# One hybrid decoder step on one core: the last layer's down projection with 512 weight columns moving past stationary activations

## The chip, the core and the metric

The kernel runs on one NeuronCore of a Trainium2 chip. TensorE (PE in the rows, with its weight loads as PEld) multiplies, VectorE (DVE), ScalarE (ACT) and GpSimd (POOL) work on vectors, SyncE (SP) issues most transfers. The metric is the device time of one execution in microseconds. The kernel before takes 2923.28 us, the median of three runs (2923.02 to 2924.85).

## What is computed

The reference is one step of a two-layer decoder on 320 tokens: 256 of a prompt and 64 of eight samples. Each layer has a mixer and a feed-forward part. The part that matters here is the feed-forward of the second (last) layer, whose result is the output:

```python
def _ffn(h, w1, w2):
    a = jax.nn.relu(jnp.einsum('btd,df->btf', h, w1))
    return jnp.einsum('btf,fd->btd', a * a, w2)

y_p = y_p + _ffn(_rmsnorm(y_p, norm_ffn[li]), w_ff1[li], w_ff2[li])
y_s = y_s + _ffn(_rmsnorm(y_s, norm_ffn[li]), w_ff1[li], w_ff2[li])
```

D_MODEL is 2048 and the hidden size 8192, so w1 is 2048 x 8192 and w2 8192 x 2048, both in f32.

## The kernel before

Activations lie transposed: 128 channels on the partitions, 16 chunks of channels, and the 320 tokens (N) in the free dimension. Every f32 product is made of three products of float32r numbers (fp32r in the rows): each operand is split into a high part h and a remainder l, and l·h + h·l + h·h is summed in PSUM. xh, xl hold the hidden activations of a quarter, yh, yl the normed input of a layer, y the residual.

Weights come in units of 2 x 128 rows by 512 columns (w_dma, SP, tile wraw, four buffers). w_conv makes of each half unit (128 rows x 512 columns) whi on ACT (line 145) and wlo on DVE (line 146), six buffers each; w_fill keeps six halves converted or in use and is called once for every two halves, before their matmuls.

gemm is the loop of every large product. A group is 512 output columns in four PSUM banks of six (m = 0 to 3); for every pair of k chunks (a step of two halves) and each m it issues, per chunk, three matmuls: 128 weight columns are stationary, the 320 tokens move (lines 204 to 206). So one chunk and one group are 12 matmuls of 320 moving columns. After the last chunk of a bank comes evac. Work around it is hung on two counters: after(k, f) runs f k calls of step() later (a step() after each m), at(n, f) at slot n (side() counts one slot per pair of halves).

ffn(l, ...) goes through the hidden dimension in four quarters: up (w1, reads yh and yl, evac writes xh and xl), then down (w2, reads xh and xl). In each down, residual multiplies the bank by r1 (line 1455, DVE; r1 is the squared norm's reciprocal per token, the same on all partitions) and adds it to y (POOL at line 1459, one step later, or DVE at 1457 in the last quarter of the last layer). In that last quarter store turns each finished chunk of y: three transposes on TensorE into a bank (line 1634), a copy of the prompt's part by ACT (1635) and of the samples' by DVE (1636), and for every second chunk two transfers out (1640, 1641).

The order of every engine's instructions is the order in which the program issues them; nothing reorders them later.

Of the kernel before, what the change touches and what calls it, by code (L numbers as in the profile page):

```python
# [11 lines left out]
F32 = mybir.dt.float32  # L12
F32R = mybir.dt.float32r
I32 = mybir.dt.int32
AF = mybir.ActivationFunctionType
ALU = mybir.AluOpType
AX = mybir.AxisListType

D = 2048
NP_TOK = 256  # L20
NB = 8
NT = 8
N = NP_TOK + NB * NT
# [47 lines left out]
def tile_hybrid_step(ctx: ExitStack, tc: tile.TileContext, A, O, stop=None, dbg=None):  # L71
    nc = tc.nc
    ctx.enter_context(tc.manual_schedule())
    V, S, G, PE, SP = nc.vector, nc.scalar, nc.gpsimd, nc.tensor, nc.sync
# [8 lines left out]
    def pool(name, side="left"):  # L83
        return tc.tile_pool(name=name, bufs=1, side=side, reuse_waits="tile")

    def bank(tag):
        return psum.tile([128, 512], F32, name="ps_" + tag, tag=tag, bufs=nbank[tag])
# [39 lines left out]
    st = {"dma": 0, "conv": 0, "half": 0, "step": 0, "slot": 0, "ahead": 2}  # L127

    def w_dma():
        w, k, ku, c, width = units[st["dma"]]  # L130
        st["dma"] += 1
        r = wp.tile([128, UW], F32, name="wraw", bufs=NRAW)
        SP.dma_start(r[:, :ku * width].rearrange("p (k f) -> p k f", k=ku),
                     w[k * 128:(k + ku) * 128, c:c + width].rearrange("(k p) f -> p k f", p=128))
        raws.append(r)

    def w_conv():
        u, hf = divmod(st["conv"], 2)
        if st["dma"] == u:
            w_dma()  # L140
        st["conv"] += 1
        r = (raws.popleft() if hf else raws[0])[:, hf * HW:hf * HW + HW]
        h = wp.tile([128, HW], F32R, name="whi", bufs=NSP)
        l = wp.tile([128, HW], F32R, name="wlo", bufs=NSP)
        S.copy(h, r)  # L145
        (G if u < 4 and hf == 0 else V).tensor_tensor(l, r, h.bitcast(F32), ALU.subtract)  # L146
        convs.append((h, l))

    def w_fill():
        while st["conv"] < min(st["half"] + st["ahead"], 2 * len(units)):  # L150
            w_conv()
        while st["dma"] < min(st["conv"] // 2 + NRAW, len(units)):
            w_dma()

    def w_next():
        ku, width = units[st["half"] // 2][2::2]
        ku //= 2
        st["half"] += 1
        h, l = convs.popleft()
        return (h.rearrange("p (k f) -> p k f", k=ku), l.rearrange("p (k f) -> p k f", k=ku), ku)  # L160
# [4 lines left out]
    def at(n, f, *a):  # L165
        later.setdefault(n, deque()).append((f, a))

    def side(n=1):
        st["slot"] += n
        n = st["slot"]  # L170
        for m in sorted(k for k in later if k <= n):
            q = later.pop(m)
            while q:
                f, a = q.popleft()
                f(*a)
# [4 lines left out]
    def after(k, f):  # L180
        dq.setdefault(st["step"] + k, []).append(f)

    def step():
        st["step"] += 1
        for k in sorted(k for k in dq if k <= st["step"]):
            for f in dq.pop(k):
                f()

    def gemm(groups, nk, act, evac, width=512):

        nm = width // 128
        for g in range(groups):
            ps = [bank("g") for _ in range(nm)]
            k = 0
            while k < nk:
                for nh in (2,) if width == 512 else (1, 1):
                    w_fill()
                    ks = [(h, l, j) for h, l, n in [w_next() for _ in range(nh)] for j in range(n)]
                    ku = len(ks)
                    for m in range(nm):  # L200
                        for j, (h, l, jj) in enumerate(ks):
                            ah, al = act(k + j)
                            wh, wl = h[:, jj, m * 128:(m + 1) * 128], l[:, jj, m * 128:(m + 1) * 128]
                            PE.matmul(ps[m][:, :N], wh, al, start=k + j == 0, stop=False)  # L204
                            PE.matmul(ps[m][:, :N], wl, ah, start=False, stop=False)  # L205
                            PE.matmul(ps[m][:, :N], wh, ah, start=False, stop=k + j == nk - 1)  # L206
                        if k + ku == nk:
                            evac(g, m, ps[m])
                        step()
                    k += ku  # L210
                side()
                yield

    def run(gen):
        for _ in gen:
            pass

    def drain():
        while dq:
            step()  # L220
# [3 lines left out]
    ident = cm[:, C_ID:C_ID + 128]  # L224
# [45 lines left out]
    tn = [128, 128, 64]  # L270
# [150 lines left out]
    def norm_begin():  # L421
        nacc["t"] = misc.tile([128, N], F32, name="nacc", bufs=2)
        nacc["n"] = 0
# [518 lines left out]
    for bp in range(4):  # L942
        for i in range(2):
            n = CN + 8 * bp + 4 * i
# [16 lines left out]
    for b in "sw":  # L961
        n = E["k" + b]
# [4 lines left out]
    for g in range(4):  # L967
        n = E[f"q{g}"]
# [4 lines left out]
    n = CN + 34  # L973
# [384 lines left out]
    for pr in range(4):  # L1358
        n = C0 + 8 * pr
# [14 lines left out]
    for b in range(NB + 1):  # L1374
        n = P4 + 3 * b
# [21 lines left out]
    actp = ctx.enter_context(ExitStack())  # L1397
    act = actp.enter_context(pool("act"))

    xh = act.tile([128, 16, N], F32R, name="xh")  # L1400
    xl = act.tile([128, 16, N], F32R, name="xl")
    y = ctx.enter_context(pool("ypl")).tile([128, 16, N], F32, name="y")
    for c in range(4):
        SP.dma_start(y[:, 4 * c:4 * c + 4], xt_d[:, 4 * c:4 * c + 4])
# [3 lines left out]
    n = st["slot"]  # L1408
# [28 lines left out]
    misc = ctx.enter_context(pool("misc", "right"))  # L1437
    r1 = misc.tile([128, N], F32, name="r1")
# [10 lines left out]
    def residual(ps, c, nxt, scale=None, last=False):  # L1449

        if scale is None:
            V.tensor_tensor(y[:, c], ps[:, :N], y[:, c], ALU.add)
        else:
            t = misc.tile([128, N], F32, name="rs", bufs=3)
            V.tensor_tensor(t, ps[:, :N], scale, ALU.mult)  # L1455
            if last or nxt is not None:
                V.tensor_tensor(y[:, c], y[:, c], t, ALU.add)
            else:
                after(1, lambda: G.tensor_tensor(y[:, c], y[:, c], t, ALU.add))  # L1459
        if nxt is not None:  # L1460
            if c == 0:
                norm_begin()

            gn = par[:, nxt + c:nxt + c + 1]

            def lo():
                V.scalar_tensor_tensor(yl[:, c], y[:, c], gn, yh[:, c].bitcast(F32), op0=ALU.mult, op1=ALU.subtract)

            after(1, lambda: S.activation(yh[:, c], y[:, c], AF.Copy, scale=gn))
            after(2, lambda: norm_add(y[:, c]))  # L1470
            after(3, lo)

    def after_norm(dst, squared):
        n = st["slot"]
        at(n + 2, norm_end, dst, squared)
# [2 lines left out]
        drain()  # L1478
        run(gemm(4, 16 - k0, lambda k: xact(k0 + k), lambda g, m, ps: residual(ps, 4 * g + m, nxt)))

    def ffn(l, nxt, last=None):
        def up(g, m, ps):
            c = 4 * g + m
            t = misc.tile([128, N], F32, name="fr", tag="fr", bufs=5)
            S.activation(t, ps[:, :N], AF.Relu)  # L1485

            def lo():
                V.tensor_tensor(t, t, t, ALU.mult)  # L1488
                V.tensor_tensor(xl[:, c], t, xh[:, c].bitcast(F32), ALU.subtract)  # L1489

            after(1, lambda: S.activation(xh[:, c], t, AF.Square))  # L1491
            after(3, lo)

        for qt in range(4):
            if qt == 0:
                drain()
                after_norm(r1, True)
            run(gemm(4, 16, yact2, up))
            drain()
            end = qt == 3  # L1500

            def down(g, m, ps):
                done = end and last is not None
                residual(ps, 4 * g + m, nxt if end else None, r1, done)
                if done:
                    after(3, lambda: last(4 * g + m))

            run(gemm(4, 16, xact, down))
        drain()

    GFF, GMX = GF, GM
    for qt in range(4):
# [108 lines left out]
        return  # L1621


    outp = ctx.enter_context(pool("outp"))
    yt = {}

    def store(c):
        q = c // 4
        if c % 4 == 0:
            yt[q] = outp.tile([128, 3, 512], F32, name="yt", bufs=2)  # L1630
        t = yt[q]
        p = bank("a")
        for i in range(3):
            PE.transpose(p[:tn[i], 128 * i:128 * i + 128], y[:, c, 128 * i:128 * i + tn[i]], ident)
        S.copy(t[:, 0:2, 128 * (c % 4):128 * (c % 4) + 128], p[:, :256].rearrange("p (i d) -> p i d", i=2))
        V.tensor_copy(t[:64, 2, 128 * (c % 4):128 * (c % 4) + 128], p[:64, 256:384])
        if c % 2:
            f = slice(128 * (c % 4) - 128, 128 * (c % 4) + 128)
            d = slice(128 * c - 128, 128 * c + 128)
            SP.dma_start(O[0][0].rearrange("(i p) d -> p i d", p=128)[:, :, d], t[:, 0:2, f])  # L1640
            SP.dma_start(O[1].rearrange("b t d -> (b t) d")[:, d], t[:64, 2, f])

    ffn(1, None, store)


# [28 lines left out]
```

## Time and profile before

| | us |
|---|---|
| median of three runs | 2923.28 |
| the profiled execution, device time | 2929.41 |
| its span (first to last instruction) | 2927.6 |
| TensorE matmul busy | 2872.9 (98%) |
| TensorE weight load busy | 2802.8 (96%) |
| VectorE busy | 1583.7 (54%) |
| ScalarE busy | 1256.6 (43%) |
| GpSimd busy | 285.6 (10%) |

The last layer's feed-forward takes the end of the span, from about 2015 us on. In the timeline a row has the start, the time taken, the engine, the line, the operation and its tiles; for a matmul `128*128 128x320` is the stationary tile (partitions * columns) and the moving one. Matmuls are pipelined: one shown with 0.31 us overlaps the next, and what counts is the distance from one start to the next. A merged row (x8) runs from the first start to the last end.

### The profile page before, as it was taken

Reading aid. Unit: us, or ns where it says so; the run is one execution under the profiler, and the core shown is the slowest. Engines: PE = TensorE matmul, PEld = TensorE weight load, DVE = VectorE, ACT = ScalarE, POOL = GpSimd, SP = SyncE. Lnnn points to the kernel's source line nnn. Section 1 sums busy time; section 2 is a strip of 40 time slices with the busy share of each in tenths; the row PEclk is TensorE's granted clock in tenths of the full one; section 3 lists DMA queues with packets and bytes.
Section 4 is the critical chain, followed back from the end, with each engine's and each line's share of the span. In section 5 each row is a group of like instructions: output and inputs, shape, how many; then the busy total and the mean of one; then the engine's idle time right before and its main releaser. Section 6 shows DMA issues by size and latency. Waiting matters only on the chain.

```text
span 2927.6 us, 53019 instructions
## 1 busy us (share of the span) xinstructions
PE 2872.9 (98%) x20723; PEld 2802.8 (96%) x20723; DVE 1583.7 (54%) x2913; ACT 1256.6 (43%) x2370; POOL 285.6 (10%) x449
## 2 busy tenths in 40 slices
PE   9998998999999999999999999999999999999999
PEld 8887777899999999999999999999999999999999
DVE  6676676665545444444565555555444444544544
ACT  5665754444434434433444333344433433433433
POOL 1103321020010010010010111111011011001000
PEclk9999999999999999999999999999999999999999
DMA  8765247645455555545444444444545544444543
GB/s 242 213 202 149 73 142 227 218 139 149 161 166 165 159 163 161 166 159 165 149 147 153 151 148 149 151 148 148 153 149 148 150 150 153 149 149 150 149 157 120
DMA packets 284826, 463.94 MB, mean 158 GB/s; under 512 B 18666, under 2 KB 112598, under 8 KB 284047
## 3 DMA queue, kind: packets, MB, share of 16 engines
q1 hardware_dynamic: 281886, 453.68, 50.4%
q0 software_dynamic: 2640, 6.85, 0.7%
q8 instruction: 162, 2.65, 0.4%
q14 instruction: 90, 0.73, 0.1%
q10 hardware_dynamic: 48, 0.02, 0.0%
HBM read 452.95 MB, written 15.92 MB: 160 GB/s over the span
## 4 chain that ended last, share of the span: by engine, by line
PE 85%; DVE 5%; ACT 3%; DMA 2%; issue 2%; SPq 2%; POOL 0%; ACTq 0%; DVEq 0%; POOLq 0%
PE ps_g L204 27%; PE ps_g L205 27%; PE ps_g L206 27%; DVE wlo L146 1%; DVE hrs L833 1%; SPq L659 1%; ACT cy L702 1%; SPq L684 1%; ACT whi L145 1%; DMA xn<-in_x_prompt_dram 1%; PE ps_a L1165 0%; DMA cx<-in_cache_cmp_v_dram 0%; DMA wraw<-in_w_in_e_dram 0%; ACT ps L1090 0%; PE ps_a L1289 0%
## 5 line engine op out<-in xcount | busy, mean ns | idle before, releaser
L146 DVE TENSOR_TENSOR wlo<-wraw,whi 128x512 fp32r<-128x512 f32 x1488 | 1000.0, 712 | 1158.8 <-ACT whi L145 1157.2
L145 ACT CAST whi<-wraw 128x512 fp32r<-128x512 f32 x1492 | 853.0, 618 | 1364.4 <-PE ps_g L206 1330.0
L204 PE MATMUL ps_g<-yl,whi 128*128 128x320 f32 x3408 | 1067.8, 313 | 12.2 <-DVE kv L816 7.8
L206 PE MATMUL ps_g<-yh,whi 128*128 128x320 f32 x3408 | 1057.7, 310 | 0.0
L205 PE MATMUL ps_g<-yh,wlo 128*128 128x320 f32 x3408 | 1057.6, 310 | 0.0
L204 PE MATMUL ps_g<-xl,whi 128*128 128x320 f32 x2560 | 795.9, 311 | 1.2 <-DVE xl L446 1.2
L206 PE MATMUL ps_g<-xh,whi 128*128 128x320 f32 x2560 | 792.1, 309 | 0.0
L205 PE MATMUL ps_g<-xh,wlo 128*128 128x320 f32 x2560 | 792.0, 309 | 0.0
L204 PEld LDWEIGHTS ps_g<-yl,whi 128*128 128x128 f32 x3408 | 644.3, 189 | 22.7 <-DVE kv L816 8.3
L205 PEld LDWEIGHTS ps_g<-yh,wlo 128*128 128x128 f32 x3408 | 644.4, 189 | 1.5
L206 PEld LDWEIGHTS ps_g<-yh,whi 128*128 128x128 f32 x3408 | 643.9, 189 | 0.0
L204 PEld LDWEIGHTS ps_g<-xl,whi 128*128 128x128 f32 x2560 | 482.0, 188 | 2.3 <-DVE xl L446 1.4
L205 PEld LDWEIGHTS ps_g<-xh,wlo 128*128 128x128 f32 x2560 | 481.9, 188 | 0.0
L206 PEld LDWEIGHTS ps_g<-xh,whi 128*128 128x128 f32 x2560 | 481.6, 188 | 0.0
L1459 POOL TENSOR_TENSOR y<-y,rs 128x320 f32<-128x320 f32 x96 | 92.3, 994 | 1257.8 <-DVE rs L1455 1257.8
L1455 DVE TENSOR_TENSOR rs<-ps_g,r 128x320 f32<-128x320 f32 x128 | 60.7, 488 | 25.4 <-PE ps_g L206 24.3
L1488 DVE TENSOR_TENSOR fr<-fr 128x320 f32<-128x320 f32 x128 | 62.2, 486 | 11.1 <-ACT xh L1491 11.1
L702 ACT COPY cy<-cx 64x1024 f32<-64x1024 f32 x32 | 65.3, 2042 | 0.6
L1489 DVE TENSOR_TENSOR xl<-fr,xh 128x320 fp32r<-128x320 f32 x128 | 63.0, 492 | 4.4
L1491 ACT ACTIVATE xh<-fr 128x320 fp32r<-128x320 f32 x128 | 60.4, 472 | 4.0
L431 POOL TENSOR_TENSOR nacc<-nacc,nsq 128x320 f32<-128x320 f32 x45 | 44.1, 981 | 171.9 <-ACT nsq L427 170.3
L1485 ACT ACTIVATE fr<-ps_g 128x320 f32<-128x320 f32 x128 | 56.0, 437 | 5.7 <-PE ps_g L206 5.7
(382 smaller groups left out, 1340.7 us busy)
## 6 DMA issues: line engine op xcount, KB each, us to landing
wraw<-in_w_ff_dram SPq DMA_DIRECT2D x512, 512.0 KB, 3.7
wraw<-in_w_in_o_dram SPq DMA_DIRECT2D x96, 512.0 KB, 4.9
wraw<-in_w_in_e_dram SPq DMA_DIRECT2D x74, 512.0 KB, 5.1
wraw<-in_w_out_e_dram SPq DMA_DIRECT2D x32, 512.0 KB, 4.6
wraw<-in_w_out_o_dram SPq DMA_DIRECT2D x32, 512.0 KB, 4.4
cx<-in_cache_cmp_k_dram SPq DMA_DIRECT2D x64, 128.0 KB, 2.2
cx<-in_cache_cmp_v_dram SPq DMA_DIRECT2D x64, 128.0 KB, 2.9
kl<-in_cache_sel_k_dram SPq DMA_DIRECT2D x64, 128.0 KB, 2.4
```

Of the source, the lines that this page charges most:

```text
L145: S.copy(h, r)
L146: (G if u < 4 and hf == 0 else V).tensor_tensor(l, r, h.bitcast(F32), ALU.subtract)
L204: PE.matmul(ps[m][:, :N], wh, al, start=k + j == 0, stop=False)
L205: PE.matmul(ps[m][:, :N], wl, ah, start=False, stop=False)
L206: PE.matmul(ps[m][:, :N], wh, ah, start=False, stop=k + j == nk - 1)
L702: (S.copy if k % 2 else V.tensor_copy)(y[64 * half:64 * half + 64, :, s_], v[64 * s_:64 * s_ + 64, :, half].rearrange("p n d -> p d n"))
L1455: V.tensor_tensor(t, ps[:, :N], scale, ALU.mult)
L1459: after(1, lambda: G.tensor_tensor(y[:, c], y[:, c], t, ALU.add))
L1485: S.activation(t, ps[:, :N], AF.Relu)
L1488: V.tensor_tensor(t, t, t, ALU.mult)
L1489: V.tensor_tensor(xl[:, c], t, xh[:, c].bitcast(F32), ALU.subtract)
L1491: after(1, lambda: S.activation(xh[:, c], t, AF.Square))
```

## The change

In the last layer alone, down becomes gemm_t with the roles exchanged. The tokens' activations are stationary, 128 columns at a time, and a converted half unit (128 rows x 512 weight columns) moves. The result has tokens on the partitions: bank 0 is prompt tokens 0 to 127, bank 1 tokens 128 to 255, bank 2 the samples. xh and xl become two halves of one tile xhl, and in the last layer xl holds its 64 sample columns first, so that the samples' h and l stand side by side (columns 256 to 383): one stationary tile of 64 + 64 columns, past which wlo and then whi move, so that partitions 0 to 63 of bank 2 collect the sums with h and 64 to 127 those with l. One chunk and one group are then 3 + 3 + 2 = 8 matmuls of 512 moving columns, in three banks.

The residual is turned at the start of the layer's feed-forward instead of at the end: z_of makes three transposes, an ACT copy and a DVE copy for each of 16 chunks, one per slot, beside the first quarter's up; r_col turns r1 into a column rc. down_t is the evac: for each of banks 0 and 1 one DVE operation z = bank · rc + z of 128x512, and for bank 2 in two halves an ACT copy of the upper 64 partitions and two such DVE operations of 64x256. In the last quarter a transfer out follows each piece of z. The POOL adds and line 1455 of this layer's down are gone, and the transposes, copies and transfers of store. In up the write of xl is two operations (256 and 64 columns).

```diff
-    xh = act.tile([128, 16, N], F32R, name="xh")
-    xl = act.tile([128, 16, N], F32R, name="xl")
+    xhl = act.tile([128, 16, 2 * N], F32R, name="xhl")
+    xh, xl = xhl[:, :, :N], xhl[:, :, N:]
...
+                for o, q, n in ((64, 0, NP_TOK), (0, NP_TOK, 64)):
+                    V.tensor_tensor(xl[:, c, o:o + n], t[:, q:q + n], xh[:, c, q:q + n].bitcast(F32), ALU.subtract)
...
-            run(gemm(4, 16, xact, down))
+            run(gemm(4, 16, xact, down) if down_t is None else gemm_t(down_t, end))
...
+    def gemm_t(evac, end):
+
+        for g in range(4):
+            ps = [bank("g") for _ in range(3)]
+            for u in range(8):
+                w_fill()
+                for k in (2 * u, 2 * u + 1):
+                    h, l, _ = w_next()
+                    h, l = h[:, 0], l[:, 0]
+                    for t in range(2):
+                        s_ = slice(128 * t, 128 * t + 128)
+                        PE.matmul(ps[t], xl[:, k, 64 + 128 * t:192 + 128 * t], h, start=k == 0, stop=False)
+                        PE.matmul(ps[t], xh[:, k, s_], l, start=False, stop=False)
+                        PE.matmul(ps[t], xh[:, k, s_], h, start=False, stop=k == 15)
+
+                    for w, e in ((l, False), (h, k == 15)):
+                        PE.matmul(ps[2], xhl[:, k, NP_TOK:N + 64], w, start=k == 0 and w is l, stop=e)
+                if u == 7:
+                    evac(g, ps, end)
+                step()
+                side()
+                yield
...
+    def turn():
+        n = st["slot"]
+        for c in range(16):
+            at(n + 1 + c, z_of, c)
+        at(n + 18, r_col)
+
+    def down_t(g, ps, end):
+        f = slice(512 * g, 512 * g + 512)
+        for t in range(2):
+            V.scalar_tensor_tensor(z[:, t, f], ps[t], rc[:, t:t + 1], z[:, t, f], op0=ALU.mult, op1=ALU.add)
+            if end:
+                SP.dma_start(O[0][0, 128 * t:128 * t + 128, f], z[:, t, f])
+        for k in range(0, 512, 256):
+            c = misc.tile([128, N], F32, name="rs", bufs=3)
+            S.copy(c[:64, :256], ps[2][64:128, k:k + 256])
+            fk = slice(512 * g + k, 512 * g + k + 256)
+            zs = z[:64, 2, fk]
+            V.scalar_tensor_tensor(zs, ps[2][:64, k:k + 256], rc[:64, 2:3], zs, op0=ALU.mult, op1=ALU.add)
+            V.scalar_tensor_tensor(zs, c[:64, :256], rc[:64, 2:3], zs, op0=ALU.mult, op1=ALU.add)
+            if end:
+                SP.dma_start(O[1].rearrange("b t d -> (b t) d")[:, fk], zs)
```

On TensorE, in the last layer's last down, before (names: the tile written <- the two operands, then the size of the moving tile; here at a group's end, where the transposes of store stand between):

```order
L204 MATMUL ps_g<-xl,whi 128x320
L205 MATMUL ps_g<-xh,wlo 128x320
L206 MATMUL ps_g<-xh,whi 128x320
L1634 MATMUL ps_a<-cm,y 128x128 x2
L1634 MATMUL ps_a<-cm,y 64x128
L204 MATMUL ps_g<-xl,whi 128x320
```

On TensorE, at the start of the last layer's first down, now (eight rows are one chunk of k):

```order
L1526 MATMUL ps_g<-whi,xhl 128x512
L1527 MATMUL ps_g<-wlo,xhl 128x512
L1528 MATMUL ps_g<-whi,xhl 128x512
L1526 MATMUL ps_g<-whi,xhl 128x512
L1527 MATMUL ps_g<-wlo,xhl 128x512
L1528 MATMUL ps_g<-whi,xhl 128x512
L1531 MATMUL ps_g<-wlo,xhl 128x512
L1531 MATMUL ps_g<-whi,xhl 128x512
```

Twelve rows of 128x320 have become eight of 128x512, and no transpose stands in the down any more; the transposes have the same three matmuls each, at line 1658, between the rows of the first up.

On VectorE, the end of the program before (wlo is the conversion of weights, rs and y the residual, yt the copy for the output):

```order
L146 TENSOR_TENSOR wlo<-wraw,whi 128x512 x10
L1455 TENSOR_TENSOR rs<-ps_g,r_8781 128x320
L1457 TENSOR_TENSOR y<-y,rs 128x320
L1455 TENSOR_TENSOR rs<-ps_g,r_8781 128x320
L1457 TENSOR_TENSOR y<-y,rs 128x320
L1455 TENSOR_TENSOR rs<-ps_g,r_8781 128x320
L1457 TENSOR_TENSOR y<-y,rs 128x320
L1636 COPY yt<-ps_a 64x128
L1455 TENSOR_TENSOR rs<-ps_g,r_8781 128x320
L1457 TENSOR_TENSOR y<-y,rs 128x320
L1636 COPY yt<-ps_a 64x128 x3
```

On VectorE, the end of the program now:

```order
L1688 SCALAR_TENSOR_TENSOR z<-rs,rc,z 64x256
L146 TENSOR_TENSOR wlo<-wraw,whi 128x512 x12
L1679 SCALAR_TENSOR_TENSOR z<-ps_g,rc,z 128x512 x2
L1687 SCALAR_TENSOR_TENSOR z<-ps_g,rc,z 64x256
L1688 SCALAR_TENSOR_TENSOR z<-rs,rc,z 64x256
L1687 SCALAR_TENSOR_TENSOR z<-ps_g,rc,z 64x256
L1688 SCALAR_TENSOR_TENSOR z<-rs,rc,z 64x256
```

The evac of a group is now one block of six operations behind the last step's conversions; before, it was spread over the four banks of the step. The same block ends every group of the four downs.

## Rows read from the trace of the kernel before

**Rows 1.** The page: engines (busy us, share, instructions) and the chain that ended last.

```profile
PE 2872.9 (98%) x20723; PEld 2802.8 (96%) x20723; DVE 1583.7 (54%) x2913; ACT 1256.6 (43%) x2370; POOL 285.6 (10%) x449
...
PE 85%; DVE 5%; ACT 3%; DMA 2%; issue 2%; SPq 2%; POOL 0%; ACTq 0%; DVEq 0%; POOLq 0%
```

**Rows 2.** Stretches: us; PE, PEld, DVE, ACT, POOL busy (count); PEclk; DMA share; GB/s.

```profile
2100.00:2800.00 700.00, 700.00 (x4775) 700.00 (x4774) 336.02 (x547) 268.42 (x497) 46.16 (x48) 1.00 0.48 150
```

**Rows 3.** The stretch of the last feed-forward, tile xl alone: PE, PEld, DVE.

```profile
2022.23:2921.28 899.05, 317.49 (x1024) 192.22 (x1024) 31.48 (x64) 1.00 0.48 149
```

**Rows 4.** Timeline in the last down: matmuls and weight loads.

```profile
2880.33 0.31 PE L204 MATMUL ps_g<-xl,whi 128*128 128x320 f32 x1
2880.34 0.19 PEld L205 LDWEIGHTS ps_g<-xh,wlo 128*128 128x128 f32 x1
2880.48 0.31 PE L205 MATMUL ps_g<-xh,wlo 128*128 128x320 f32 x1
2880.62 0.31 PE L206 MATMUL ps_g<-xh,whi 128*128 128x320 f32 x1
2880.77 0.31 PE L204 MATMUL ps_g<-xl,whi 128*128 128x320 f32 x1
```

**Rows 5.** An early stretch at half clock, and TensorE's timeline in it.

```profile
40.20:43.20 3.00, 3.00 (x13) 3.00 (x12) 1.18 (x2) 0.62 (x1) 0.00 (x0) 0.50 0.78 227
...
40.65 0.47 PE L206 MATMUL ps_g<-yh,whi 128*128 128x320 f32 x1
40.92 0.47 PE L204 MATMUL ps_g<-yl,whi 128*128 128x320 f32 x1
41.19 0.47 PE L205 MATMUL ps_g<-yh,wlo 128*128 128x320 f32 x1
```

**Rows 6.** Timeline of TensorE: plain f32 matmuls of 320 columns, then transposes.

```profile
458.28 1.24 PE L583 MATMUL ps_a<-xc,wab 128*128 128x320 f32 x4
459.35 1.58 PE L1289 MATMUL ps_a<-cm,sp 128*128 128x128 f32 x13
```

**Rows 7.** Timeline: a float32r matmul ahead of a weight load of nine columns.

```profile
609.02 0.31 PE L206 MATMUL ps_g<-xh,whi 128*128 128x320 f32 x1
609.17 0.38 PE L633 MATMUL ps_a<-cm,hl_o 128*9 128x128 f32 x2
...
609.03 0.23 PEld L633 LDWEIGHTS ps_a<-cm,hl_o 128*9 128x9 f32 x2
```

**Rows 8.** Timeline: 512 moving columns in f32, two stationary tiles of 64 columns side by side.

```profile
420.55 0.14 PEld L1247 LDWEIGHTS ps_a<-ktl,qbd 128*64 128x64 f32 x2 [0.28 <-issue]
420.98 0.14 PEld L1247 LDWEIGHTS ps_a<-ktl,qbd 128*64 128x64 f32 x2 [0.28 <-issue]
```

**Rows 9.** Timeline of TensorE around one turned chunk in the last down.

```profile
2862.05 0.31 PE L206 MATMUL ps_g<-xh,whi 128*128 128x320 f32 x1
2862.20 0.49 PE L1634 MATMUL ps_a<-cm,y 128*128 128x128 f32 x3
2862.45 0.39 PE L204 MATMUL ps_g<-xl,whi 128*128 128x320 f32 x1
2862.68 0.30 PE L205 MATMUL ps_g<-xh,wlo 128*128 128x320 f32 x1
2862.82 0.31 PE L206 MATMUL ps_g<-xh,whi 128*128 128x320 f32 x1
```

**Rows 10.** Groups in 2800 to 2928 us: busy us, mean ns; idle before, releaser.

```profile
L146 DVE TENSOR_TENSOR wlo<-wraw,whi 128x512 fp32r<-128x512 f32 x62 | 40.0, 687 | 55.5 <-ACT whi L145 55.5
L1455 DVE TENSOR_TENSOR rs<-ps_g,r 128x320 f32<-128x320 f32 x16 | 7.7, 481 | 6.4 <-PE ps_g L206 6.4
L1636 DVE COPY yt<-ps_a 64x128 f32<-64x128 f32 x16 | 4.4, 277 | 1.3 <-ACT yt L1635 1.3
...
L145 ACT CAST whi<-wraw 128x512 fp32r<-128x512 f32 x62 | 35.4, 619 | 58.6 <-PE ps_g L206 58.6
L1635 ACT COPY yt<-ps_a 128x256 f32<-128x256 f32 x16 | 6.0, 373 | 22.9 <-PE ps_a L1634 22.9
```

**Rows 11.** Timeline at the end of the program: TensorE, VectorE, SP's queue.

```profile
2918.17 0.31 PE L206 MATMUL ps_g<-xh,whi 128*128 128x320 f32 x1
...
2918.51 0.49 DVE L1455 TENSOR_TENSOR rs<-ps_g,r 128x320 f32<-128x320 f32 x1 [6.41 <-PE ps_g L206]
...
2921.13 0.31 PE L206 MATMUL ps_g<-xh,whi 128*128 128x320 f32 x1
...
2923.74 0.28 DVE L1636 COPY yt<-ps_a 64x128 f32<-64x128 f32 x1 [0.83 <-ACT yt L1635]
...
2924.21 0.47 SPq L1641 DMA_DIRECT2D out_dram<-yt  x1
```

More of the change, by code (lines that the diff above doesn't have):

```diff
@@ L1479, in out_proj, with ffn @@
         run(gemm(4, 16 - k0, lambda k: xact(k0 + k), lambda g, m, ps: residual(ps, 4 * g + m, nxt)))
-    def ffn(l, nxt, last=None):
+    def ffn(l, nxt, turn=None, down_t=None):
         def up(g, m, ps):
@@ L1488, in lo @@
                 V.tensor_tensor(t, t, t, ALU.mult)
-                V.tensor_tensor(xl[:, c], t, xh[:, c].bitcast(F32), ALU.subtract)
+                if down_t is None:
+                    V.tensor_tensor(xl[:, c], t, xh[:, c].bitcast(F32), ALU.subtract)
+                    return
+                for o, q, n in ((64, 0, NP_TOK), (0, NP_TOK, 64)):
+                    V.tensor_tensor(xl[:, c, o:o + n], t[:, q:q + n], xh[:, c, q:q + n].bitcast(F32), ALU.subtract)
             after(1, lambda: S.activation(xh[:, c], t, AF.Square))
@@ L1497, in ffn @@
                 after_norm(r1, True)
+                if down_t is not None:
+                    turn()
             run(gemm(4, 16, yact2, up))
@@ L1502, in down @@
             def down(g, m, ps):
[L1503 to L1506, printed above, removed]
-            run(gemm(4, 16, xact, down))
-        drain()
+                residual(ps, 4 * g + m, nxt if end else None, r1)
+            run(gemm(4, 16, xact, down) if down_t is None else gemm_t(down_t, end))
+        drain()
+    def gemm_t(evac, end):
[18 more added lines that the diff above has]
+                yield
     GFF, GMX = GF, GM
@@ L1621, in tile_hybrid_step, with z_of @@
         return
[L1624 to L1631, printed above, removed]
+    outp = ctx.enter_context(pool("outp", "right"))
+    z = outp.tile([128, 3, D], F32, name="z")
+    rc = outp.tile([128, 3], F32, name="rc")
+    def z_of(c):
         p = bank("a")
@@ L1634, in store, with r_col @@
             PE.transpose(p[:tn[i], 128 * i:128 * i + 128], y[:, c, 128 * i:128 * i + tn[i]], ident)
[L1635 to L1643, printed above, removed]
+        f = slice(128 * c, 128 * c + 128)
+        S.copy(z[:, 0:2, f], p[:, :256].rearrange("p (i d) -> p i d", i=2))
+        V.tensor_copy(z[:64, 2, f], p[:64, 256:384])
+    def r_col():
+        p = bank("a")
+        for i in range(3):
+            PE.transpose(p[:tn[i], 128 * i:128 * i + 128], r1[:, 128 * i:128 * i + tn[i]], ident)
+        V.tensor_copy(rc[:, 0:2], p[:, 0:256:128])
+        V.tensor_copy(rc[:64, 2:3], p[:64, 256:257])
+    def turn():
[18 more added lines that the diff above has]
+                SP.dma_start(O[1].rearrange("b t d -> (b t) d")[:, fk], zs)
+    ffn(1, None, turn, down_t)
 _INS = ['x_prompt', 'x_sample', 'cache_cmp_k', 'cache_cmp_v', 'cache_sel_k', 'cache_sel_v', 'cache_win_k',
```

## The prediction

> **What bounds the kernel now.** I read the page first: TensorE is busy 98% of the span and stands for 85% of the chain that ended last, VectorE 54%, ScalarE 43% [rows 1]. So I look for what sets TensorE's pace. The table of stretches shows 4775 matmuls in 700 us [rows 2]: one starts every 146.6 ns, and the timeline shows the same step by step, 2880.33, .48, .62, .77, with each weight load starting together with the matmul before its own [rows 4]. I take 146.67 ns (352 cycles of 2.4 GHz; the granted clock of the stretch is 1.00). VectorE and ScalarE wait for TensorE there, not it for them: ScalarE's conversions are idle 58.6 us in the last 128 us until a matmul frees a buffer [rows 10]. So the change is worth what it does to the matmul stream, plus what it does to the end of the program.
>
> **Number of matmuls.** The last layer's four downs are 4 quarters x 4 groups x 16 chunks = 256 pieces of 12 matmuls, 3072. The trace agrees: 1024 of the stretch read xl, one in three [rows 3]. They take 3072 x 0.14667 = 450.6 us. Now there are 256 x 8 = 2048, each with 512 moving columns. In columns alone that is more: 4096 for 3840, because the samples' tile carries l beside h and multiplies wlo by l too, which nobody needs. So the gain must come from what a matmul costs beside its columns. The two are even at 450.6 / 2048 = 220.0 ns for a matmul.
>
> **What a matmul of 512 columns costs.** No row of before shows a float32r matmul of another size than 320. At 2.4 GHz 512 columns are 213.3 ns; on top comes what the 320 show beyond 133.3 ns, namely 13.3 ns. What is it?
> At half clock (granted 0.50, the 1.2 GHz level) the same matmuls start 0.27 us apart, 40.65, 40.92, 41.19 [rows 5]: 320 / 1.2 = 266.7, nothing beyond the columns. So the columns themselves cost no extra when the array is slow; the 13.3 ns appear only where a float32r matmul streams a column per cycle of 2.4 GHz.
> It isn't the weight load: the float32r matmul at 609.02 has a load of nine columns beside it, and the next matmul starts at 609.17, 0.15 us later all the same [rows 7].
> It isn't a cost of every matmul either: four plain f32 records of 320 columns, at two cycles a column, go from 458.28 to 459.35, 1.07 us or 268 ns each where the columns take 266.7 [rows 6]; two records of 512 side by side take 0.43 us where two times 213.3 are 426.7 [rows 8].
> Two readings are left. **Fixed:** 13.3 ns (32 cycles) for each float32r matmul, whatever its length, something like a start of its stream that the slower modes hide. Then 512 columns cost 226.67 ns, and 2048 of them 464.2 us: +13.7. **In proportion:** a tenth on every column at full speed; 234.67 ns, 480.6 us: +30.0. The bound from below is the f32 row: 2 ns beyond the columns, 215.5 ns, 441.3 us: -9.2. I take the fixed one: rows 6 and 8 show extras that do not grow with the columns (1 to 3 ns at 320 and at 512 alike), and an extra that hides wholly at half clock is easier to have once per instruction than at every tenth column. Both other values stay as ends of the range's cases.
>
> The Trainium skill ("TensorE: Matmul & The Clock Gate", section "Back-to-back issue gap") gives a warm gap of N / 2.4 + 2.5 ns, 216 ns at 512 columns. By it the sum would be 2048 x 0.2158 = 442 us, 8.6 less than now; but for 320 columns it gives 136 ns and this trace shows 146.67 in [rows 4], so it does not hold for float32r as it stands.
>
> **Turning.** One turned chunk, three transposes, stretches the time between two matmuls of line 206 that have two others between them from 0.44 us (three steps) to 0.77 (2862.05 to 2862.82) [rows 9]: 0.33 us. Before, 13 of the 16 lay in the stream of the last down (three came behind the last matmul): 13 x 0.33 = 4.3. Now all 16, and one for rc, lie in the first up: 17 x 0.33 = 5.6, if their copies keep up; a chunk comes every 3.5 us, and its two copies take 0.37 and 0.28 us [rows 10]. **+1.3 us.**
>
> **The end.** Before, the last float32r matmul started at 2921.13, so its stream ended near 2921.28, and the span ends at 2927.6: 6.3 us for the last residual, three turned chunks and the last two transfers [rows 11]. Now no transposes follow. From the end of the stream: a bank can be read 0.19 us later (2918.17 + 0.15 to 2918.51 [rows 11]); banks 0 and 1 are finished five and two matmuls earlier, so that VectorE is through with the first 512-column operation and in the second. The samples' part then is an ACT copy (0.37, the copy of 128x256) and VectorE's four operations of 64x256, each between 0.28 (64x128) and 0.48 us (128x320) [rows 10], the first of which waits for the copy: 0.19 + 0.37 + 4 x 0.36 = 2.0. Before, the last copy ended at 2924.02 and the span 3.6 us later, with SP's issue at 2924.21 and the landing [rows 11]; the same follows now: 5.6. **-0.7 us.**
>
> **What I cost at nothing.** Each group's evac is now a block on VectorE: two operations of 128x512 (0.69 to 0.78 us each, from 687 ns for 128x512 and 481 scaled from 320) and the four above, 2.5 to 3.5 us in all [rows 10]. Queued behind it on VectorE are the next conversions (wlo), on ScalarE behind its two copies whi, and on SP, in the last quarter, weight transfers behind four transfers out. TensorE has two steps converted ahead, 2 x 16 x 0.227 = 7.3 us. Of that the block uses about 2 us past the end of the group's stream and the two conversions 1.4: it stays covered by some 3.5 us. Banks are three of six for each group, so the next group finds free ones. The DVE write of xl in two pieces adds 64 small operations to an engine that is idle half of the time; POOL's 48 adds and line 1455 go, off the path. Weights move in the same 256 transfers.
>
> **The sum.** +13.7 + 1.3 - 0.7 = +14.3 us. These are differences within the profiled execution (2929.41 us, with a span of 2927.6 and 1.8 around it); the median of the runs is 6.1 us or 0.2% lower, and I put the difference on it: 2923.3 + 14.3 = 2937.6, **2938 us**, 0.5% slower.
>
> **Rivals.**
> 1. *The extra vanishes at 512 columns* (the page's formula, or any floor of about 147 ns under a float32r matmul that 512 columns exceed). As a mechanism here: the 13.3 ns are not a cost of the stream but a least distance of two starts, and the columns cost 2 ns extra as in [rows 6]. For it: 146.67 ns is seen at one size alone. Against it: thirteen transposes of 128 columns take 1.58 us in all, less than 122 ns each [rows 6], so the floor would have to be float32r's own. -9.2 + 1.3 - 0.7 makes 2914.7 us, faster. It decides below 220 ns a matmul.
> 2. *The extra grows with the columns.* 234.67 ns, +30.0 + 1.3 - 0.7: 2953.9 us. For it: 352 cycles are exactly 1.1 x 320 as well as 320 + 32. Against it: what is said above on half clock.
> 3. *The block at the group's end is not covered*, and TensorE waits for wlo at the start of every group. It decides where VectorE is over 3.5 us later than I count; each us beyond costs 16 us over 16 groups: 2954 us for one. Against it: VectorE's idle time (55.5 of 128 us [rows 10]).
> 4. *It comes out even*: an extra of 5 to 8 ns, halfway between the readings: 2920 to 2926 us.
> That the stream would not change at all is no rival: the order of the instructions has the 2048 matmuls of 512 columns.
>
> **How the numbers follow.** The fixed extra 0.60, in proportion 0.17, vanishing 0.14, block not covered 0.04, halfway 0.05. The likeliest gives 2938, its own range 2933 to 2942 (the end and the turning are each good to a us or two). Together with rivals 2 and 3 that is 0.81, so the range runs from 2933 to 2956. A measurement of this kernel tells some 0.2% (5.8 us) from no change: faster by more 0.14, within 0.05, slower 0.81.
>
> **What would show it.** In the timeline of the changed kernel's last downs the starts at lines 1526 to 1531 stand 226.7 ns apart; 215 would be rival 1, 234.7 rival 2. The last layer's first up has transposes at line 1658 with some 0.33 us each chunk. TensorE has no idle time before line 1526 at a group's start; idle time there released by VectorE would be rival 3. From the last matmul to the end of the span there are 5 to 6 us. I am wrong in kind if the distance is below 220 ns, and in size if it is above 230 or if TensorE waits.

## The result and the profile after

The changed kernel takes 2938.52 us (median of 5, 2935.54 to 2944.33) against 2924.73 us (2923.02 to 2927.64) for the kernel before on the same chip: a ratio of 1.0051 [1.0036, 1.0065], 13.8 us slower by the medians and 14.8 by the means. 2938 was predicted, 2933 to 2956 as the range.

First the engines and the chain of the page, against [rows 1], then one of TensorE's new groups (busy us, mean ns, idle before):

```profile
PE 2881.6 (98%) x19702; PEld 2731.7 (93%) x19702; DVE 1601.1 (55%) x2995; ACT 1275.2 (43%) x2402; POOL 239.2 (8%) x401
...
PE 88%; DVE 4%; ACT 3%; issue 2%; DMA 2%; SPq 2%; POOL 0%; ACTq 0%; DVEq 0%; POOLq 0%
...
L1527 PE MATMUL ps_g<-wlo,xhl 128*128 128x512 f32 x512 | 199.4, 389 | 0.0
```

A thousand instructions fewer, the same 98%, a longer span: TensorE is the bound as before, and each matmul of the new kind takes longer. The mean of 389 ns is the length of one pipelined matmul, not its cost; the cost is the distance of two starts, in the timeline of a down that was turned round (start, time taken), against [rows 4]:

```profile
2199.99 0.39 PE L1526 MATMUL ps_g<-whi,xhl 128*128 128x512 f32 x1
2200.22 0.39 PE L1527 MATMUL ps_g<-wlo,xhl 128*128 128x512 f32 x1
2200.45 0.39 PE L1528 MATMUL ps_g<-whi,xhl 128*128 128x512 f32 x1
2200.68 0.39 PE L1531 MATMUL ps_g<-wlo,xhl 128*128 128x512 f32 x1
```

Starts are 226 to 227 ns apart, throughout. The program divides at its stages, so the account can be made stage by stage. First the kernel before (stretch in us; its length; busy us and count of PE, PEld, DVE, ACT, POOL; granted clock; DMA share; GB/s): first up, first down, last down.

```profile
2014.89:2128.07 113.18, 113.18 (x773) 113.02 (x771) 59.93 (x99) 50.88 (x100) 3.61 (x4) 1.00 0.50 149
2128.07:2240.71 112.64, 112.64 (x771) 112.64 (x770) 53.26 (x84) 37.81 (x68) 12.88 (x14) 1.00 0.46 150
2803.91:2921.28 117.37, 117.37 (x809) 116.67 (x808) 56.67 (x107) 39.51 (x76) 0.00 (x0) 1.00 0.42 137
```

The same stages of the changed kernel, with the second up as the third row:

```profile
2009.86:2128.57 118.71, 118.71 (x823) 118.39 (x822) 65.23 (x129) 54.71 (x115) 3.60 (x4) 1.00 0.47 142
2128.57:2244.65 116.08, 116.08 (x515) 96.19 (x513) 56.46 (x93) 41.99 (x73) 0.00 (x0) 1.00 0.47 146
2244.65:2357.28 112.63, 112.63 (x769) 112.63 (x768) 56.60 (x109) 49.59 (x96) 0.00 (x0) 1.00 0.52 150
2814.71:2930.79 116.08, 116.08 (x514) 95.95 (x512) 53.69 (x89) 39.48 (x69) 0.00 (x0) 1.00 0.45 139
```

| stage | before | after | difference |
|---|---|---|---|
| first up (now with the turning) | 113.18 | 118.71 | +5.53 |
| first, second and third down, each | 112.64 | 116.08 | +3.44, three times 10.32 |
| the three other ups | 112.64 | 112.63 | 0 |
| last down (before with the turning) | 117.37 | 116.08 | -1.29 |
| from the end of the stream to the end of the span | 6.3 | 5.9 | -0.5 |
| sum | | | +14.1 |

From the start of the last layer's feed-forward to the end of the span it is 912.7 us before (2014.89 to 2927.6) and 926.8 now (2009.86 to 2936.6), the same 14.1. The two profiled spans differ by only 9.0, because everything ahead of this feed-forward, which the change leaves alone, came out 5.0 us shorter in this one execution. Two executions differ there by a few us anyway, so a difference is made from the start of the stage on, not from the spans.

Who waits now? The waits of 2009.86 to 2936.65 (engine, line and what was waited for; us in all, times, longest) begin like this, and TensorE is in none of the rows:

```profile
DVE wlo L146 <- ACT whi L145: 402.6, 309, 2.3
ACT whi L145 <- PE ps_g L1531: 237.8, 204, 1.5
ACT whi L145 <- PE ps_g L206: 204.7, 92, 2.7
```

### The profile page after: what moved, and what is told of

It is laid out like the page before. It is cut to its first block, busy times and chain, and to the rows that moved or that the text cites. A ratio compares the mean times of both kernels' runs of the same rounds, so it can differ in the third digit from the quotient of the medians.

```text
span 2936.6 us, 50962 instructions
## 1 busy us (share of the span) xinstructions
PE 2881.6 (98%) x19702; PEld 2731.7 (93%) x19702; DVE 1601.1 (55%) x2995; ACT 1275.2 (43%) x2402; POOL 239.2 (8%) x401
## 4 chain that ended last, share of the span: by engine, by line
PE 88%; DVE 4%; ACT 3%; issue 2%; DMA 2%; SPq 2%; POOL 0%; ACTq 0%; DVEq 0%; POOLq 0%
PE ps_g L204 23%; PE ps_g L206 23%; PE ps_g L205 23%; PE ps_g L1531 4%; PE ps_g L1527 4%; PE ps_g L1526 4%; PE ps_g L1528 4%; DVE wlo L146 1%; ACT cy L702 1%; PE ps_a L712 1%; ACT whi L145 1%; SPq L1147 1%; PE ps_a L1165 1%; SPq L659 0%; DMA wraw<-in_w_in_e_dram 0%
## 5 line engine op out<-in xcount | busy, mean ns | idle before, releaser
L145 ACT CAST whi<-wraw 128x512 fp32r<-128x512 f32 x1492 | 862.8, 618 | 1280.3 <-PE ps_g L206 1005.1
L204 PE MATMUL ps_g<-xhl,whi 128*128 128x320 f32 x1536 | 477.8, 311 | 1.2 <-DVE xhl L446 1.2
L205 PE MATMUL ps_g<-xhl,wlo 128*128 128x320 f32 x1536 | 475.5, 310 | 0.0
L206 PE MATMUL ps_g<-xhl,whi 128*128 128x320 f32 x1536 | 475.4, 309 | 0.0
L204 PEld LDWEIGHTS ps_g<-xhl,whi 128*128 128x128 f32 x1536 | 288.7, 188 | 2.3 <-DVE xhl L446 1.4
L205 PEld LDWEIGHTS ps_g<-xhl,wlo 128*128 128x128 f32 x1536 | 288.7, 188 | 0.0
L206 PEld LDWEIGHTS ps_g<-xhl,whi 128*128 128x128 f32 x1536 | 288.6, 188 | 0.0
L1527 PE MATMUL ps_g<-wlo,xhl 128*128 128x512 f32 x512 | 199.4, 389 | 0.0
L1526 PE MATMUL ps_g<-whi,xhl 128*128 128x512 f32 x512 | 199.4, 389 | 0.0
L1528 PE MATMUL ps_g<-whi,xhl 128*128 128x512 f32 x512 | 199.2, 389 | 0.0
L1526 PEld LDWEIGHTS ps_g<-whi,xhl 128*128 128x128 f32 x512 | 96.1, 188 | 19.9
L1528 PEld LDWEIGHTS ps_g<-whi,xhl 128*128 128x128 f32 x512 | 96.1, 188 | 19.9
L1527 PEld LDWEIGHTS ps_g<-wlo,xhl 128*128 128x128 f32 x512 | 96.2, 188 | 19.8
L1531 PE MATMUL ps_g<-whi,xhl 128*128 128x512 f32 x256 | 99.8, 390 | 0.0
L1531 PE MATMUL ps_g<-wlo,xhl 128*128 128x512 f32 x256 | 99.8, 390 | 0.0
```

What stands on the lines that cost most here:

```text
L1526: PE.matmul(ps[t], xl[:, k, 64 + 128 * t:192 + 128 * t], h, start=k == 0, stop=False)
L1527: PE.matmul(ps[t], xh[:, k, s_], l, start=False, stop=False)
L1528: PE.matmul(ps[t], xh[:, k, s_], h, start=False, stop=k == 15)
L1531: PE.matmul(ps[2], xhl[:, k, NP_TOK:N + 64], w, start=k == 0 and w is l, stop=e)
```

## Experiments

The theory (A1): a float32r matmul at full clock costs its columns at 2.4 GHz and 13.3 ns more, once, whatever its length. Rivals: the extra grows with the columns; it comes from matmuls that follow each other into one bank; it belongs to every matmul that the columns' time doesn't hide, not to float32r; and part of the loss has to do with the layout of xhl or with the block on VectorE. Runs 1 to 6 are one execution each. They are read by their stages, which repeat to 0.01 us where nothing in them was changed, and not by their totals, which differ by a few us from one execution to the next.

**1. Other sizes.** In bank 0 each matmul becomes two of 256 columns (all but the first of a group):

```diff
+    cut = 256 if t == 0 else 512
...
-    PE.matmul(ps[t], xh[:, k, s_], l, ...)
+    for o in range(0, 512, n):
+        PE.matmul(ps[t][:, o:o + n], a, w[:, o:o + n], ...)
```

> The changed kernel, with bank 0's matmuls cut into two of 256 moving columns (only the first of a group stays whole). Theory A, a fixed 13.3 ns on every float32r matmul: pieces of 256 start 106.7 + 13.3 = 120.0 ns apart, the whole ones of 512 stay at 226.7; bank 0 costs 6 x 120 - 3 x 226.7 = 40 ns more in each of 256 chunks, about +10 us on the changed kernel, 2948 us. Rival, the extra is a twentieth to a tenth of the columns: 112 to 117 ns. Rival, the distance of short matmuls is set by the 128-column weight load (111.7 ns in the rows of 8 columns): 112 ns, some 2 to 4 us less than A.

Measured: 2955.51 us. TensorE's timeline of one chunk (an x2 row holds two pieces):

```profile
2199.87 0.40 PE L1530 MATMUL ps_g<-whi,xhl 128*128 128x256 f32 x2
2200.10 0.40 PE L1530 MATMUL ps_g<-wlo,xhl 128*128 128x256 f32 x2
...
2200.81 0.40 PE L1530 MATMUL ps_g<-wlo,xhl 128*128 128x512 f32 x1
2201.05 0.39 PE L1530 MATMUL ps_g<-whi,xhl 128*128 128x512 f32 x1
2201.28 0.40 PE L1533 MATMUL ps_g<-wlo,xhl 128*128 128x512 f32 x1
```

The pieces cost about 120 ns (2199.87 to 2200.10 for two; mean 118.8), as A1 has it. But from the start of a whole one to the next start it is 228 to 236 ns (mean 232.2), where it had been 226.7, and the chunk got 60 ns longer instead of 40. So the run is 17 us over the changed kernel where 10 were expected. That is neither reading in full, and doesn't settle it: the mixture does something itself. So the next has no mixture.

**2. Pieces of 256 only.** The same cut for all three banks.

> The changed kernel with nearly all matmuls of the downs cut into two of 256 moving columns, so that no whole ones stand between. In the mixed run the pieces stood 118.5 ns apart on the mean and the whole ones after them 233; a chunk came to 1872 ns, 59 more than uncut, where a fixed 13.3 ns gives 40. Theory A, fixed: 120.0 ns in the pure stream, a down takes 116.1 x 1920 / 1813 = 122.8 us. Rival, at 256 columns something else binds (the load of the stationary tile beside a full-rate stream): 123 to 126 ns, 126 to 129 us a down.

Measured: 2963.88 us. A down, and its timeline:

```profile
2127.24:2250.01 122.77, 122.77 (x1015) 122.25 (x1013) 56.64 (x93) 41.81 (x73) 0.00 (x0) 1.00 0.41 139
...
2199.88 0.40 PE L1531 MATMUL ps_g<-wlo,xhl 128*128 128x256 f32 x2
2200.12 0.40 PE L1531 MATMUL ps_g<-whi,xhl 128*128 128x256 f32 x2
```

Two pieces take 0.24 us, 120.0 each. At 256, 320 and 512 columns the columns take 106.7, 133.3 and 213.3 ns at 2.4 GHz, and the starts are 120.0, 146.67 and 226.67 apart: 13.3 more each time. A tenth on every column would give 117.3 at 256, and any extra in proportion to the columns would leave the down as long as with 512 (a chunk has the same 4096 columns); it is 6.7 us longer. The fixed extra is shown for three sizes. Why wholes behind pieces cost 5.5 ns more in the mixture stays open.

**3. Banks in turn.** The eight matmuls of a chunk in the order bank 0, 1, 2, 0, 1, 2, 0, 1, so that no two in a row add into the same bank:

```diff
+    PE.matmul(ps[0], xl[:, k, c[0]], h, ...)
+    PE.matmul(ps[1], xl[:, k, c[1]], h, ...)
+    PE.matmul(ps[2], xhl[:, k, NP_TOK:N + 64], l, ...)
+    PE.matmul(ps[0], xh[:, k, b[0]], l, ...)
...
```

> The changed kernel, with the eight matmuls of a chunk in another order, so that no two in a row add into the same PSUM bank. Theory A, the 13.3 ns are in the float32r stream itself: 226.7 ns as before, 2938 us. Rival, they are a wait of the next matmul for the bank that the one before it still adds into: 215.5 ns, 2048 x 11.2 = 23 us less, 2916 us.

Measured: 2935.05 us, near the changed kernel's lowest (2935.54), and its down is the same to the hundredth:

```profile
2124.50:2240.58 116.08, 116.08 (x515) 96.13 (x513) 54.92 (x92) 42.25 (x74) 0.00 (x0) 1.00 0.46 146
```

The bank has no part in the extra.

**4. The layout alone.** The kernel before, with xh and xl as halves of one tile and the split write of xl:

```diff
-    xh = act.tile([128, 16, N], F32R, name="xh")
-    xl = act.tile([128, 16, N], F32R, name="xl")
+    xhl = act.tile([128, 16, 2 * N], F32R, name="xhl")
+    xh, xl = xhl[:, :, :N], xhl[:, :, N:]
```

> The kernel before, with xh and xl as halves of one tile and, in the last layer, the write of xl in two pieces (256 and 64 tokens); nothing else. Costed at nothing: within 3 us of the kernel before, and the last layer's down stages stay at 112.64 us. Rival, one tile for both adds waits, or the extra writes come late: TensorE idle at the start of a down, some tenths of a us in each of four quarters.

Measured: 2924.53 us, the kernel before 2923.3 beside it. First up and last down:

```profile
2010.01:2123.18 113.17, 113.17 (x772) 113.01 (x771) 60.75 (x111) 50.89 (x99) 3.60 (x4) 1.00 0.49 149
2799.02:2916.39 117.37, 117.37 (x809) 116.68 (x808) 56.88 (x111) 39.52 (x76) 0.00 (x0) 1.00 0.41 137
```

Both are as long as in the kernel before. VectorE has 12 operations more in the first up's stretch (x111 for x99) and nobody waits for them. So of the +5.5 us in the changed kernel's first up nothing is the split write; the turning remains.

**5. The block made longer, by a little.** Behind each group's evac VectorE does eight more operations of 128x320, whose results nobody uses:

```diff
+    for _ in range(4):
+        x = misc.tile([128, N], F32, name="fr", tag="fr", bufs=5)
+        V.tensor_tensor(x, y[:, 0], y[:, 1], ALU.mult)
+        V.tensor_tensor(x, x, x, ALU.mult)
```

> The changed kernel, with eight more operations of 128x320 on VectorE (some 3.7 us, results unused) behind each group's evac block. In the trace of the changed kernel the block ends 2.4 us into the next group and the wlo that TensorE needs next is ready 4.3 us early, so theory A (the block is covered, with some 4 us to spare): the three first downs stay at 116.1 us and TensorE never waits; the end of the program may come up to 1 us later. Rival, the cover is thinner than that (the queue behind adds to it): some 0.5 to 2 us of idle TensorE at each group's start, 8 to 30 us in all.

Measured: 2943.14 us. The down still takes 116.08, with 24 more operations in VectorE's count (three of its four blocks lie inside the stretch):

```profile
2131.87:2247.95 116.08, 116.08 (x515) 96.13 (x514) 66.37 (x117) 41.99 (x73) 0.00 (x0) 1.00 0.45 146
```

Eight operations are 3.7 us, at 0.47 each, and the cover takes them. They cost only behind the last matmul: from its start to the end of the span it is 7.5 us, in the changed kernel 6.1. The other 3.3 us of the 4.6 over the changed kernel's median lie ahead of the first down (it starts at 2131.87, there at 2128.57), where the two kernels are the same.

**6. The block made longer, by much.** The same with `range(10)`, twenty operations, 9.3 us.

> The same with twenty more operations (some 8.5 to 9.5 us). Theory A: the cover of 4.3 us is used up and TensorE waits for wlo some 4 to 5 us at the start of 15 groups (ups too, where the quarter's last block stands): 60 to 75 us more than the changed kernel, about 3005 us. Rival, conversions catch up within the group from further ahead: no more than 20 us.

Measured: 3058.04 us, 119.5 more than the changed kernel; 60 to 75 were expected. The waits from 2009 us on, then a pause in TensorE's timeline, the granted clock of two stretches around it, and the first down:

```profile
PEld ps_g L1527 <- DVE wlo L146: 62.8, 12, 5.2
PE ps_g L1527 <- DVE wlo L146: 57.7, 12, 4.8
...
PEld ps_g L205 <- DVE wlo L146: 16.1, 3, 5.4
PE ps_g L205 <- DVE wlo L146: 15.3, 3, 5.1
...
2166.45 0.39 PE L1526 MATMUL ps_g<-whi,xhl 128*128 128x512 f32 x1
2171.65 0.79 PE L1527 MATMUL ps_g<-wlo,xhl 128*128 128x512 f32 x1 [4.81 <-DVE wlo L146]
2172.24 0.63 PE L1528 MATMUL ps_g<-whi,xhl 128*128 128x512 f32 x1
2172.67 0.63 PE L1526 MATMUL ps_g<-whi,xhl 128*128 128x512 f32 x1
...
2160.00:2166.00 6.00, 6.00 (x29) 4.95 (x27) 5.75 (x14) 3.17 (x6) 0.00 (x0) 1.00 0.04 13
2171.60:2176.50 4.90, 4.85 (x11) 3.80 (x12) 3.70 (x6) 0.62 (x1) 0.00 (x0) 0.50 0.49 153
...
2130.16:2268.25 138.09, 123.66 (x514) 100.70 (x513) 82.45 (x153) 41.96 (x73) 0.00 (x0) 0.94 0.39 123
```

This is rival 3 made to happen. In each of 15 groups (twelve in the downs, three where the next up begins) TensorE uses up the two steps that were converted ahead, 7.3 us of work in a down, and then waits about 5 us for wlo, which stands behind VectorE's block. Here 9.3 us of block make 5.0 us of pause (2166.45 + 0.23 to 2171.65), so the spare cover of the changed kernel is 4.3 us. The fifteen pauses make 75 us, counted from where the next matmul was due (the rows give 73 for the matmuls and 79 for their loads, which start earlier). What was not expected is the second price: behind each pause the granted clock is 0.50, the 1.2 GHz level, for 7 to 14 matmuls of 512 columns that start 0.43 us apart (in the ups 12 to 23 of 320). That costs 2.3 us more for each pause on the mean, 35 in all. Another 7 us stand behind the last matmul, where the span's end waits for the last block; these make 117 of the 119.5. At the lower level 512 columns take 426.7 ns and the starts are 0.43 apart: nothing is added there, as in [rows 5] for 320.

**7. Two of the three products in bf16.** The kernel before, in whose last-layer downs the products xl·whi and xh·wlo have operands rounded to bf16 (xb holds xl and xh so, and ScalarE makes whb beside whi), while xh·whi stays float32r; the same sizes, banks and order. This changes the arithmetic of these two products.

```diff
+    PE.matmul(ps[m][:, :N], hb[:, f], xb[0][:, c, :N], ...)
+    PE.matmul(ps[m][:, :N], l[:, f], xb[0][:, c, N:], ...)
     PE.matmul(ps[m][:, :N], h[:, f], xh[:, c], ...)
```

> The kernel before, with the two small products (l x h and h x l) of the last layer's down in bf16 and the large one (h x h) in float32r as before; ScalarE makes a bf16 copy of each converted weight half, VectorE one of xh. Theory A1, the 13.3 ns belong to a stream of four-byte columns at one column per cycle: the bf16 matmuls of 320 columns start 135.5 ns after each other, the float32r ones keep 146.7; 2048 x 11.2 = 23 us less than the kernel before, 2902 us. Theory A2, they belong to any matmul at full rate, or to accumulating in turn: 146.7 for all, 2925 us, no change. Rival, a change of number format between matmuls costs by itself: slower than 2925 us.

Measured: 2917.89 us (2913.87 to 2919.78), 0.9976 [0.9967, 0.9986] of the kernel before (2923.3); about a quarter of the gain that A1 expects. TensorE and its weight loads:

```profile
2200.27 0.31 PE L242 MATMUL ps_g<-xb,whb 128*128 128x320 bf16 x1
...
2200.42 0.30 PE L243 MATMUL ps_g<-xb,wlb 128*128 128x320 bf16 x1
2200.42 0.19 PEld L244 LDWEIGHTS ps_g<-xh,whi 128*128 128x128 f32 x1
2200.45 0.41 PE L244 MATMUL ps_g<-xh,whi 128*128 128x320 f32 x1
2200.70 0.10 PEld L242 LDWEIGHTS <-whb 128*128 128x128 bf16 x1
2200.70 0.31 PE L242 MATMUL ps_g<-xb,whb 128*128 128x320 bf16 x1
```

Three take 0.43 us, where 146.7 and twice 135.8 would be 418 and the kernel before has 440. In [rows 4] each load starts with the matmul ahead of its own. Here the four-byte load does so too (2200.42), but the load of whb, behind the float32r matmul, starts only with its own matmul (both 2200.70). The bf16 matmul with this late load stands 146 ns ahead of the next one, where run 8 has 136 within a row of bf16. So the change of format within the stream has a price, about 15 ns for each three, and 10 of them go with the late load. The length of a bf16 matmul alone can't be read from this run.

**8. The same with the formats apart.** In each step of two chunks the sixteen bf16 matmuls stand first, then the eight float32r.

> As bf16low, but in each step the sixteen bf16 matmuls of the four banks come first and then the eight float32r ones, so that the number format changes twice in a step and not sixteen times. bf16low's three matmuls took 433 ns where three float32r ones take 440 and two of 135.5 with one of 146.7 would take 418. Theory A1, bf16 columns carry 2 ns and each change of format some 8 to 15: the bf16 matmuls stand 135.5 ns apart within their row, a step takes 16 x 135.5 + 8 x 146.7 + 2 x 15 = 3.37 us for 3.52, 128 steps make 19 us less than the kernel before, 2904 us. Theory A2, the 13.3 ns come with any matmul at one column per cycle: 146 ns within the row as well, and the 7 us that bf16low gains come from elsewhere: 2917 us or more.

Measured: 2910.82 us (2909.78 to 2914.27), 0.9956 [0.9939, 0.9972] of the kernel before (2924.89). TensorE's timeline, with one of its weight loads, and a down:

```profile
2200.03 0.30 PE L242 MATMUL ps_g<-xb,whb 128*128 128x320 bf16 x1
...
2200.17 0.30 PE L243 MATMUL ps_g<-xb,wlb 128*128 128x320 bf16 x1
2200.17 0.10 PEld L242 LDWEIGHTS <-whb 128*128 128x128 bf16 x1
2200.31 0.30 PE L242 MATMUL ps_g<-xb,whb 128*128 128x320 bf16 x1
...
2125.02:2232.53 107.51, 107.51 (x770) 86.20 (x769) 55.89 (x89) 69.13 (x129) 12.79 (x13) 1.00 0.47 157
```

The bf16 starts are 135 to 136 ns apart, mean 135.9: 2.6 beyond the columns. The down is 32 steps of 16 x 135.9 + 8 x 146.7 = 3.35 us, 107.1; measured 107.5, 12 ns more in each step with its two changes of format. Operands of two bytes, with the same columns and banks, don't have the 13.3 ns: they belong to float32r. The loads are shorter here as well (0.10 us for 0.19), so the matmul and its load are not told apart. The distance of the bf16 starts fits the Trainium skill ("TensorE: Matmul & The Clock Gate", section "Back-to-back issue gap"), whose warm gap of N / 2.4 + 2.5 ns gives 135.8 at 320 columns; for float32r the runs contradict it at all three sizes. Of the 19 us expected 14 came by the medians: the three first downs bring 5.1 each, but the last only 1.5 (117.37 to 115.92), since TensorE waits in it for VectorE.

**9. The best of it.** As run 8, but in the last step of a group bank by bank, so that the four evacs are spread again.

> As bf16grp, but in the last step of a group each bank's six matmuls stand together, so that the four evacs are spread over the step again. In bf16grp the last down took 115.8 us where the three others took 107.5, with TensorE waiting for VectorE in its last steps. Theory: the three first downs stay near 107.6, the last comes to some 112 us (107.6 and 13 turned chunks at 0.33); 5 x 3 + 5 = 20 us less than the kernel before, 2904 us. Rival: the spread formats cost in those 16 steps what the evacs gain, 2909 us.

Measured: 2908.38 us (2905.03 to 2910.7), 0.9937 [0.9924, 0.9951] of the kernel before (2925.71). First and last down:

```profile
2126.72:2234.40 107.68, 107.68 (x770) 85.66 (x769) 56.28 (x90) 69.12 (x129) 13.67 (x14) 1.00 0.47 157
2787.66:2902.46 114.80, 112.41 (x810) 90.24 (x809) 60.96 (x113) 71.34 (x138) 0.00 (x0) 1.00 0.42 141
```

It is 17 us under the kernel before, and ahead of the changed one by 30. Three downs bring 5.0 us each (112.64 to 107.68). The last brings only 2.6, since TensorE stands idle for 2.4 us of it (114.80 against 112.41 busy). The waits from 2787 us on name the turning's transposes, which wait for the residual on VectorE:

```profile
PE ps_a L1687 <- DVE y L1503: 2.4, 3, 0.8
```

A form in which wlo goes past the samples' h alone, so that the wasted quarter of bank 2 goes, was not tried on the chip.

## Why the prediction was right

- **Matmuls, +13.7 predicted.** Each of four downs is 3.44 us longer, without the turning: +13.8. The step that decided was "I take the fixed one", and run 2 shows that it holds: 13.3 ns at 256, 320 and 512. No row of before could decide it, and to that extent it was luck. Its first argument, that the extra of other kinds doesn't grow with the columns, was weak (those rows are of other modes); the second, that it vanishes at half clock, was borne out again at 512 columns in run 6. What the extra is, inside the chip, no run shows: "something like a start of its stream" is still only a picture. Nor is it told apart whether the matmul or its own four-byte load has it. "It isn't the weight load" went too far: in [rows 7] only the load of the matmul behind is a short one.
- **The 4096 columns.** Of the balance, 256 columns more for each chunk and group are 106.7 ns and four matmuls fewer are 53.3 ns: 256 x 53.3 ns is the +13.7. The samples' tile, of whose four parts three are needed, costs more than the fewer starts bring.
- **Turning, +1.3.** Measured +0.8: the first up got 5.5 longer as counted (17 x 0.33 = 5.6), but the last down lost 4.7, not 4.3. Thirteen chunks had cost 0.36 each there, and I had read one. Run 4 shows that the rest of the first up's edits is free.
- **The end, -0.7.** Measured -0.5. The steps are seen in the timeline of the end of the changed kernel, against [rows 11]:

```profile
2930.56 0.39 PE L1531 MATMUL ps_g<-whi,xhl 128*128 128x512 f32 x1
...
2930.99 0.37 ACT L1684 COPY rs<-ps_g 64x256 f32<-64x256 f32 x1 [10.26 <-PE ps_g L1531]
2931.39 0.48 DVE L1687 SCALAR_TENSOR_TENSOR z<-ps_g,rc,z 64x256 f32<-64x256 f32 x1
2931.90 0.37 ACT L1684 COPY rs<-ps_g 64x256 f32<-64x256 f32 x1 [0.54 <-DVE z L1687]
...
2932.81 0.47 DVE L1688 SCALAR_TENSOR_TENSOR z<-rs,rc,z 64x256 f32<-64x256 f32 x1
```

  Two errors offset each other in part. The four operations of 64x256 take 0.48 us each, the upper of my two bounds (I took 0.36), so VectorE ends 2.5 us behind the stream (2930.79 to 2933.28) and not 2.0. From there to the end of the span it is 3.4 us and not 3.6. The second copy waits for VectorE's operation on the same bank, which I had not seen, but it ends at 2932.27, ahead of the operation that reads it (2932.81).
- **The block on VectorE, 0.** Right, with 4.3 us of spare cover in place of 3.5: TensorE has no wait, run 5 adds 3.7 us and finds none, run 6 adds 9.3 and finds 5.0, just where the two steps counted as converted ahead end. Rival 3's price was too low, though: a us beyond the cover costs its wait in 15 groups, but a pause of 5 us also costs the clock behind it.
- **The sum.** 13.8 + 0.8 - 0.5 = 14.1 for 14.3. That the median came within a us of 2938 is luck in part: the five runs of the changed kernel spread over 9 us.
- **Rivals.** 1 (215.5 ns), 2 (234.7) and 4 (about 220) all fall with 226.7 in the first timeline; 3 falls with the waits, among which TensorE has none.

## What to carry to other kernels

Before one turns a matmul round for fewer and longer instructions, count both sides: starts saved times the extra per start, read from the trace (13.3 ns here), against the columns added, padding of odd tiles too; here 53 ns against 107. Where a format's extra is the cost, the format is the larger lever: two bf16 products of three brought 17 us, if the result may be that much coarser and matmuls of one format stand together. And a block moved onto another engine is free just as long as the bound engine's lead; measure that lead by making the block longer.

## What was not expected of the hardware

- A float32r matmul has 13.3 ns beyond its columns at full clock (120.0, 146.7 and 226.7 ns at 256, 320 and 512 columns) and none at half clock (0.43 us at 512); a bf16 one has 2.6 at 320.
- Changing between bf16 and float32r within the stream costs some 15 ns for three matmuls (433 for 418). The load of a bf16 matmul right behind a float32r one starts with its own matmul and not with the one ahead.
- Whole float32r matmuls of 512 among pieces of 256 take 232.2 ns to the next start, on the mean, where a stream of wholes alone has 226.7. Why is open.
- After pauses of 5 us the granted clock is 0.50 for 7 to 14 matmuls of 512 columns, so that a pause of 5 us costs over 7.
- VectorE's fused multiply-add from a bank takes 0.48 us on 64x256 and 0.75 on 128x512: a quarter of the elements, but nearly two thirds of the time.
